# Two activation tiles placed 64 bytes aside from the spacing of the others, in a two-block network of float32 matmuls on one core

## The chip, the cores and the metric

The kernel runs on one core of one Trainium2 chip. The metric is the time of one execution on the device in microseconds; the number for the kernel before is the median of three runs. A profile is one execution, taken apart by the hardware profiler; its span goes from the first to the last instruction, and its own time lies a little above its span.

## The reference

A token block of 256 x 1024 float32 goes through two networks, one after the other. The first has one layer: a feed-forward, a mixer (softmax attention with a forget gate beside a chunked delta rule), a cross-attention to a memory of 256 tokens, and a second feed-forward. The second has two layers: a feed-forward, a mixer (a short convolution beside a state-space scan), a feed-forward, and a gated embedding. There are six feed-forwards in all, of one form:

```python
def swiglu(x, w_gate, w_up, w_down):
    return (jax.nn.silu(x @ w_gate) * (x @ w_up)) @ w_down
```

with 1024 inputs, 2816 inner features and 1024 outputs. Nearly all of the arithmetic is in such products of the activations with weights of 1024 to 2816 rows, all float32.

## The kernel before

Activations are kept transposed: features on the 128 partitions, the 256 tokens along the row. An activation of 1024 features is eight tiles, the 2816 inner features are NF = 22 tiles. A product in full float32 is made of three products in the faster type fp32r: each operand is split into a rounded part (hi) and the rest (lo), and hi x hi, hi x lo and lo x hi are added up in PSUM.

Weights come in units of up to four blocks of 128 x 256. `wunit` (line 284) loads a unit into a tile `raw` by a DMA issued from the sync engine's queue, ScalarE rounds it into a tile `hi` (line 298), VectorE subtracts to get `lo` (line 299). There are four `raw`, three `hi` and three `lo` tiles of 4096 bytes a partition, in turns.

An activation that enters a product is split into a tile of the arena `R`: 2048 bytes a partition, the rounded part in the first 1024 bytes, the rest in the second. `mm3` (line 326) makes the three matmuls of one block: the weights are held in TensorE (128 x 128, 512 bytes of a partition), the activation streams past them (256 columns):

```python
wh, wl = (q[:, m0:m0 + P] for q in w)
xh, xl = x[:, 0, :], x[:, 1, :]
self.mm(ps, wh, xh, first, False)
self.mm(ps, wh, xl, False, False)
self.mm(ps, wl, xh, False, last)
```

All of them are recorded on line 266. `block` (line 338) goes through the K input tiles four at a time (one unit), and within the four, first for one half of 128 output features and then for the other, tile by tile. So a pass over eight input tiles is 48 matmuls, in which each tile has three in a row, twice; a pass over 22 inner tiles is 132. In `proj_tok` (two projections per mixer and memory) the roles are swapped: the activation is held and hi or lo stream. `preload` splits the first weight blocks of some stages into R tiles ahead of time, so in four short stretches both operands of a matmul are R tiles.

A feed-forward (`ffn`, line 471) makes 11 units of gate and up, 22 passes over its eight input tiles, and writes 22 inner tiles; then four passes over these for the down projection. Each matmul pass waits for its weights by semaphores; TensorE takes its instructions in the order in which the program's planner has put them.

The arena `Arena` (line 97) hands out tiles. `add` makes n tiles in a pool, named by the arena and a running number: `R` has 20 outer tiles r0 to r19 from the start, and every feed-forward opens a scope (line 459) with NF = 22 inner ones, which lie behind the outer ones in the same memory each time (r20 to r41 in the first, r42 to r63 in the second, r64 to r85 in the third, then r90, r112 and r138 and on). `get` hands out the front of the free list, `put` appends to its end, new tiles go to the front. So a feed-forward's inner activation is the 22 inner tiles in order, and its inputs are outer tiles as the free list has them.

Followed through the program, r1 is one of the eight inputs in the first, second, third and sixth feed-forward and not in the fourth and fifth, and serves for one of the inputs in other stages; 746 matmuls stream it. 144 stream the fifth inner tile of a feed-forward (24 in each).

The pools lay their tiles down one after another in each partition. By the sizes of the tiles in the order of the program (bytes from the start of a partition): the three `hi` begin at 42112, 46208 and 50304, the three `lo` at 54400, 58496 and 62592, r0 at 119104 and r1 at 121152, r19 at 158016, the first inner tile at 160064, the fifth at 168256. So `hi` and `lo`, and every 512-byte slice of them that is held, begin at a multiple of 128 (at 128 modulo 512), and every R tile begins 64 past one (at 320 modulo 512). A tile named `pad` of 32 bytes, which nothing reads or writes, stands in the constants' pool; its place in the layout stays empty.

Of the kernel before, what the change touches and what calls it, by code (L numbers as in the profile page):

```python
# [8 lines left out]
F32 = mybir.dt.float32  # L9
# [6 lines left out]
P = 128  # L16
# [4 lines left out]
NF = FF // P  # L21
# [75 lines left out]
class Arena:  # L97
# [7 lines left out]
    def add(self, pool, n):  # L105

        new = []
        for _ in range(n):
            nm = f"{self.name}{self.n}"
            new.append(pool.tile(self.shape, self.dtype, tag=nm, name=nm, bufs=1)[:])  # L110
            self.n += 1
        self.free[:0] = new
        self.parts.append(new)
# [1362 lines left out]
```

## Time and profile before

| | us |
|---|---|
| runs of the kernel before | 2220.98, 2214.37, 2216.32 |
| their median | 2216.32 |
| the profiled execution, its own time | 2218.59 |
| its span | 2216.8 |
| TensorE (PE) busy | 2195.6 |
| VectorE (DVE) busy | 1558.2 |
| ScalarE (ACT) busy | 1185.7 |
| GpSimd (POOL) busy | 43.7 |

Busy times of different engines lie beside each other and don't add up. A matmul's duration in the profile is from its start to a modelled end; matmuls are pipelined, the next starts while this one still runs, so 99% busy says that PE is never without work and not that it is at its peak. In the lists, "x1483" is a count and "281" after a busy time is the mean duration of one in ns. An entry of the form `pm<-r,hi` is a matmul into a PSUM tile pm from an R tile and a hi tile; buffer numbers are left out, so the rows don't tell r1 from r0.

### The profile page before, as it was taken

To read this page: it belongs to the slowest core of one execution; us is meant where nothing else is said; L and a number is where in the kernel's file an instruction comes from. 1 tells how busy PE (TensorE), PEld (TensorE's weight loads), DVE (VectorE), ACT (ScalarE), POOL (GpSimd) and SP (SyncE) were. 2 spreads that over 40 slices of the span, in tenths; PEclk is the share of its full clock that TensorE was granted. 3 is DMA by queue.
4 is the path that set the end of the run, shared out by engine and by line. 5 is a ranking of instruction groups with operands and counts; after the bars stand their busy time and mean duration, and the time that the engine had idled before them with its cause. 6 is when DMAs were issued, how large, how long until landed. Compare 5 with 4: busy or idle time off the path is not lost.

```text
span 2216.8 us, 45480 instructions
## 1 busy us (share of the span) xinstructions
PE 2195.6 (99%) x18672; PEld 2153.5 (97%) x18672; DVE 1558.2 (70%) x2608; ACT 1185.7 (53%) x2033; POOL 43.7 (2%) x54
## 2 busy tenths in 40 slices
PE   8999999999999999999999999999999999999998
PEld 8999997999999999998999999999999999999998
DVE  7756873667665766798766766676669876767666
ACT  6545633555444544567555555454457755645444
POOL 1000000000000000000000000000000000000000
PEclk9999997999999999999999999999999999999999
DMA  7565520535566556553455656656665436566563
GB/s 256 177 188 166 166 77 1 172 124 162 189 184 192 173 185 184 188 179 105 157 189 184 193 191 193 189 186 193 191 199 184 135 126 194 178 195 192 193 189 126
DMA packets 110369, 379.44 MB, mean 171 GB/s; under 512 B 12368, under 2 KB 17104, under 8 KB 110160
## 3 DMA queue, kind: packets, MB, share of 16 engines
q1 hardware_dynamic: 110160, 376.53, 53.6%
q8 instruction: 146, 2.39, 0.5%
q14 instruction: 63, 0.52, 0.1%
HBM read 375.43 MB, written 1.05 MB: 170 GB/s over the span
## 4 chain that ended last, share of the span: by engine, by line
PE 96%; DVE 2%; ACT 1%; DMA 1%; issue 0%; POOL 0%; SPq 0%; DVEq 0%; ACTq 0%; POOLq 0%
PE pm L266 84%; PE px L266 11%; PE px L269 1%; DVE lo L299 0%; DVE s L260 0%; DMA raw<-in_ffn_w_gate_dram 0%; DMA raw<-in_ple_w_gate_dram 0%; ACT hi L298 0%; DMA raw<-in_ffn_wu_dram 0%; ACT d L263 0%; PE pm L269 0%; ACT L263 0%; DVE r L260 0%; DVE w L254 0%; DVE w L260 0%
## 5 line engine op out<-in xcount | busy, mean ns | idle before, releaser
L266 PE MATMUL pm<-r,hi 128*128 128x256 f32 x10640 | 1864.0, 280 | 7.5 <-ACT hi L298 5.7
L266 PEld LDWEIGHTS pm<-r,hi 128*128 128x128 f32 x10640 | 1625.1, 189 | 9.8 <-ACT hi L298 5.7
L266 PE MATMUL pm<-r,lo 128*128 128x256 f32 x5320 | 1485.3, 279 | 0.0
L299 DVE TENSOR_TENSOR lo<-raw,hi 128x1024 fp32r<-128x1024 f32 (+1 forms) x718 | 860.9, 1199 | 488.9 <-ACT hi L298 485.6
L298 ACT CAST hi<-raw 128x1024 fp32r<-128x1024 f32 (+1 forms) x718 | 739.3, 1030 | 732.7 <-PE pm L266 576.7
L266 PEld LDWEIGHTS pm<-r,lo 128*128 128x128 f32 x5320 | 1002.1, 188 | 1.2 <-issue 0.7
L277 ACT CAST r<-w 128x256 fp32r<-128x256 f32 x136 | 54.5, 403 | 60.4 <-DVE w L254 60.3
L254 DVE TENSOR_TENSOR t<-pm,rb 128x512 f32<-128x512 f32 (+1 forms) x132 | 80.4, 635 | 0.2
L263 ACT ACTIVATE r<-s,vec 128x256 fp32r<-128x256 f32 x136 | 66.0, 504 | 21.4 <-DVE s L260 17.9
L263 ACT ACTIVATE sq<-s 128x256 f32<-128x256 f32 x152 | 60.4, 411 | 28.1 <-DVE s L254 19.8
L260 DVE SCALAR_TENSOR_TENSOR s<-pm,vec,s 128x255 f32<-128x255 f32 x144 | 68.9, 479 | 2.8
L260 DVE SCALAR_TENSOR_TENSOR r<-s,vec,r 128x256 fp32r<-128x256 f32 x136 | 65.3, 498 | 4.9 <-ACT r L263 4.4
L266 PE MATMUL px<-r,hi 128*128 128x256 f32 x384 | 66.9, 279 | 0.0
L278 DVE TENSOR_TENSOR r<-w,r 128x256 fp32r<-128x256 f32 x136 | 57.0, 421 | 8.1
L266 PEld LDWEIGHTS px<-r,hi 128*128 128x128 f32 x384 | 58.6, 189 | 0.0
L266 PE MATMUL px<-r,lo 128*128 128x256 f32 x192 | 53.5, 278 | 0.0
L414 POOL TENSOR_TENSOR rs<-rv,mhalf 128x2 f32<-128x2 f32 x26 | 23.4, 900 | 1505.0 <-DVE rv L412 1505.0
L263 ACT ACTIVATE w<-t 128x256 f32<-128x256 f32 x132 | 48.1, 409 | 7.2 <-DVE t L254 7.2
L254 DVE TENSOR_TENSOR w<-w,t 128x256 f32<-128x256 f32 x132 | 50.1, 418 | 0.3 <-ACT w L263 0.2
L266 PE MATMUL px<-d,d 128*64 128x128 f32 (+2 forms) x384 | 42.7, 291 | 0.3 <-DVE d L254 0.2
L257 DVE TENSOR_TENSOR acc<-acc,sq 128x256 f32<-128x256 f32 x94 | 39.4, 419 | 4.6 <-ACT sq L263 1.9
L263 ACT ACTIVATE d<-px,nac 128x128 f32<-128x128 f32 x128 | 36.5, 376 | 3.1 <-PE px L266 2.8
(231 smaller groups left out, 1369.2 us busy)
## 6 DMA issues: line engine op xcount, KB each, us to landing
raw<-in_w_in_dram SPq DMA_DIRECT2D x188, 512.0 KB, 3.7
raw<-in_ffn_wg_dram SPq DMA_DIRECT2D x88, 512.0 KB, 4.4
raw<-in_ffn_wu_dram SPq DMA_DIRECT2D x88, 512.0 KB, 4.3
raw<-in_ffn_wd_dram SPq DMA_DIRECT2D x80, 512.0 KB, 4.0
raw<-in_ffn_w_up_dram SPq DMA_DIRECT2D x44, 512.0 KB, 4.5
raw<-in_ffn_w_gate_dram SPq DMA_DIRECT2D x43, 512.0 KB, 4.5
raw<-in_ffn_w_down_dram SPq DMA_DIRECT2D x40, 512.0 KB, 3.8
raw<-in_m_w_out_dram SPq DMA_DIRECT2D x32, 512.0 KB, 4.3
```

The source lines that it names most:

```text
L254: self.nc.vector.tensor_tensor(out=out, in0=a, in1=b, op=ALU.mult)
L257: self.nc.vector.tensor_tensor(out=out, in0=a, in1=b, op=ALU.add)
L260: self.nc.vector.scalar_tensor_tensor(out=out, in0=a, scalar=s, in1=b, op0=op0, op1=op1)
L263: self.nc.scalar.activation(out, a, f, **kw)
L266: self.nc.tensor.matmul(out, lhsT=lhsT, rhs=rhs, start=start, stop=stop)
L269: self.nc.tensor.transpose(out, a, self.ident[:k, :k])
L277: nc.scalar.copy(hi, src)
L278: nc.vector.tensor_tensor(out=lo, in0=src, in1=hi, op=ALU.subtract)
L298: nc.scalar.copy(o, r)
L299: nc.vector.tensor_tensor(out=d, in0=r, in1=o, op=ALU.subtract)
L414: self.nc.gpsimd.tensor_tensor(out=r, in0=v, in1=self.mhalf[:, :2], op=ALU.pow)
```

## The change

When the arena `R` gets its 20 outer tiles, a tile of 16 float32 (64 bytes a partition) is set into the pool ahead of r1 and another ahead of r2. When it gets 22 inner tiles, one is set ahead of the fifth and another ahead of the sixth. Nothing reads or writes these tiles. So r1 and the fifth inner tile of each feed-forward stand 64 bytes further from the tile before them than the others do, and everything behind the second pad stands 128 bytes further on than it did, behind all four 256 bytes. In the new layout r1 begins at 121216, a multiple of 128 (384 modulo 512); r2 to r19 and the first four inner tiles begin 64 past one (448 modulo 512); the fifth inner tile begins at 168448, a multiple of 128 (0 modulo 512); the later ones 64 past one (64 modulo 512). `hi` and `lo`, which lie ahead of the arena, stay where they are.

```diff
@@ -105,8 +105,10 @@
     def add(self, pool, n):
 
         new = []
-        for _ in range(n):
+        for j in range(n):
             nm = f"{self.name}{self.n}"
+            if self.name == "r" and j in {20: (1, 2), NF: (4, 5)}.get(n, ()):
+                pool.tile([P, 16], F32, tag=f"pad{nm}", name=f"pad{nm}", bufs=1)
             new.append(pool.tile(self.shape, self.dtype, tag=nm, name=nm, bufs=1)[:])
             self.n += 1
         self.free[:0] = new
```

## Rows read from the trace of the kernel before

**Rows 1.** The page: the span, the busy time of each engine, and the chain of work that ended last by engine; from its 40 slices the clock that TensorE was granted, in tenths of full speed (9 is 90% or more).
```profile
span 2216.8 us, 45480 instructions
...
PE 2195.6 (99%) x18672; PEld 2153.5 (97%) x18672; DVE 1558.2 (70%) x2608; ACT 1185.7 (53%) x2033; POOL 43.7 (2%) x54
...
PEclk9999997999999999999999999999999999999999
...
PE 96%; DVE 2%; ACT 1%; DMA 1%; issue 0%; POOL 0%; SPq 0%; DVEq 0%; ACTq 0%; POOLq 0%
```

**Rows 2.** The two largest groups of PE's matmuls over the whole span, each shape by itself: names and shapes, count, busy us, mean ns of one, idle us before them and what ended it.
```profile
L266 PE MATMUL pm<-r,hi 128*128 128x256 f32 x10640 | 1864.0, 280 | 7.5 <-ACT hi L298 5.7 <-ACT r L263 1.1 <-DVE r L260 0.7
L266 PE MATMUL pm<-r,lo 128*128 128x256 f32 x5320 | 1485.3, 279 | 0.0
```

**Rows 3.** The same groups in two windows of 60 us: first 60 to 120 us (three rows, the last of them a spread of row factors), then 1300 to 1360 us (two rows).
```profile
L266 PE MATMUL pm<-r,hi 128*128 128x256 f32 x340 | 60.3, 281 | 0.0
L266 PE MATMUL pm<-r,lo 128*128 128x256 f32 x170 | 47.8, 281 | 0.0
L266 PE MATMUL px<-con,rs 128*128 128x128 f32 x2 | 0.4, 274 | 0.0
...
L266 PE MATMUL pm<-r,hi 128*128 128x256 f32 x354 | 60.2, 276 | 0.0
L266 PE MATMUL pm<-r,lo 128*128 128x256 f32 x178 | 49.1, 276 | 0.0
```

**Rows 4.** Busy time of each engine in five windows: start and end, length, then for each engine its busy us with the count of instructions that run in the window, the granted clock, the DMA engines' busy share and GB/s.
```profile
24.00:200.00 176.00, 174.62 (x1483) 174.42 (x1483) 115.97 (x165) 86.69 (x131) 1.62 (x1) 1.00 0.61 191
530.00:719.00 189.00, 188.99 (x1606) 188.79 (x1605) 124.16 (x179) 92.40 (x142) 0.70 (x1) 1.00 0.59 183
740.00:920.00 180.00, 180.00 (x1531) 180.00 (x1530) 116.20 (x156) 87.81 (x129) 2.57 (x1) 1.00 0.60 186
940.00:1009.00 69.00, 69.00 (x587) 68.80 (x586) 63.38 (x116) 46.37 (x74) 0.00 (x0) 1.00 0.57 180
1500.00:1650.00 150.00, 150.00 (x1326) 150.00 (x1325) 96.96 (x128) 73.36 (x105) 0.00 (x0) 1.00 0.63 194
```

**Rows 5.** Instructions of PE in order of time, like ones merged (start us, us, line and names, count): around 1746 us, and then around 1152 us.
```profile
1745.78 0.40 PE L266 MATMUL pm<-r,hi 128*128 128x256 f32 x2
...
1746.13 0.40 PE L266 MATMUL pm<-r,hi 128*128 128x256 f32 x2
1746.36 0.62 PE L269 MATMUL px<-con,s 128*128 128x128 f32 x4
...
1747.30 0.39 PE L266 MATMUL pm<-r,hi 128*128 128x256 f32 x2
...
1747.64 0.39 PE L266 MATMUL pm<-r,hi 128*128 128x256 f32 x2
...
1151.61 0.39 PE L266 MATMUL pm<-r,hi 128*128 128x256 f32 x2
...
1151.95 0.39 PE L266 MATMUL pm<-r,hi 128*128 128x256 f32 x2
...
1152.29 0.50 PE L266 MATMUL px<-ones,acc 128*128 128x1 f32 x4
...
1153.09 0.40 PE L266 MATMUL pm<-r,hi 128*128 128x256 f32 x2
...
1153.44 0.40 PE L266 MATMUL pm<-r,hi 128*128 128x256 f32 x2
```

**Rows 6.** The stretch in which R tiles stream past R tiles without interruption: the merged instruction list from its start to the matmul behind it, and its group in the window 1470 to 1475.7 us.
```profile
1470.12 5.92 PE L266 MATMUL pm<-r,r 128*128 128x256 f32 x48
1475.88 0.40 PE L266 MATMUL pm<-r,hi 128*128 128x256 f32 x2
...
L266 PE MATMUL pm<-r,r 128*128 128x256 f32 x47 | 5.8, 283 | 0.0
```

**Rows 7.** The group of matmuls with lo in windows around the four stretches of R against R: ahead of the undisturbed one (1465.5 to 1469.5 us), behind it (1476 to 1481 us), and behind the other three (449.6 to 452, 534.8 to 540 and 731.4 to 736 us).
```profile
L266 PE MATMUL pm<-r,lo 128*128 128x256 f32 x13 | 3.6, 276 | 0.0
...
L266 PE MATMUL pm<-r,lo 128*128 128x256 f32 x11 | 3.1, 281 | 0.0
...
L266 PE MATMUL pm<-r,lo 128*128 128x256 f32 x5 | 1.4, 281 | 0.0
...
L266 PE MATMUL pm<-r,lo 128*128 128x256 f32 x10 | 2.4, 281 | 0.0
...
L266 PE MATMUL pm<-r,lo 128*128 128x256 f32 x8 | 2.0, 281 | 0.0
```

**Rows 8.** Groups of matmuls in six windows: with hi in 1111 to 1151 and 1209 to 1275 us, with lo in 1389 to 1449 us, with hi in 1595 to 1661, 1936 to 2009 and 2012 to 2184 us.
```profile
L266 PE MATMUL pm<-r,hi 128*128 128x256 f32 x237 | 40.4, 276 | 0.0
...
L266 PE MATMUL pm<-r,hi 128*128 128x256 f32 x387 | 66.2, 276 | 0.0
...
L266 PE MATMUL pm<-r,lo 128*128 128x256 f32 x177 | 48.9, 276 | 0.0
...
L266 PE MATMUL pm<-r,hi 128*128 128x256 f32 x388 | 66.3, 276 | 0.0
...
L266 PE MATMUL pm<-r,hi 128*128 128x256 f32 x429 | 73.3, 276 | 0.0
...
L266 PE MATMUL pm<-r,hi 128*128 128x256 f32 x950 | 161.6, 276 | 0.0
```

## The prediction

> **What bounds the kernel now.** I read the page first [rows 1]: TensorE is busy for 2195.6 of 2216.8 us and the chain that ended last is 96% PE, with the granted clock at full in nearly every slice. No wait is worth removing; only the time of one matmul can move the end. Then I read the costliest matmuls [rows 2]: 15,960 of the 18,672 are the 256-column products of an activation tile (r, streamed) with weights (hi, lo, held) into one of the two PSUM pools; with the other pool and the swapped and small forms the program has 17,040. Their mean duration, 279 and 280 ns, is no price, since they are pipelined. The price is the distance from one start to the next, so I took windows with little else on PE. The reader is to see that the same instruction runs at two speeds, at the same full clock [rows 3, 4]. From 60 to 120 us the rows have a mean of 281 ns and some 510 matmuls, from 1300 to 1360 us 276 ns and 532. With the windows of [rows 4], less the 2.4 at the edges that a window counts too many (a matmul of 281 or 276 ns overlaps the next two): 180 us / 1528.6 = 117.8 ns against 150 us / 1323.6 = 113.3 ns. The difference is 4.4 ns, or 3.9%.
>
> Which speed rules isn't the work's doing: DVE, ACT and DMA are about as busy per us in the last row of [rows 4] as in the one of 180 us. The speed is kept for 180 us and more, and changes at an interruption. At 1746.4 us four transposes come between the matmuls, and the steps of three, 0.35 us before, are 0.34 us within a microsecond after; at 1152.3 us four small sums come between, and the steps go from 0.34 to 0.35 us [rows 5]. So there are two locked rhythms, call them slow and fast. Three of the six feed-forwards run slow, 24 to 200, 530 to 719 and 740 to 920 us; the later three run fast but for moments.
>
> There is a third speed. Four short stretches hold weights in R tiles and stream R tiles against them. In the undisturbed one 48 matmuls take from 1470.12 to 1475.88 us, 120.0 ns each, at a mean of 283 ns [rows 6]. What is different there is the address. By the layout told above hi and lo start at 0 modulo 128 bytes and every R tile at 64; in those stretches both operands start at 64. So equal remainders cost 120 ns, unequal ones 113.3 or 117.8 ns.
>
> **The change part by part.** It adds no instruction, wait or transfer: nothing reads or writes the pads. It puts r1, and the fifth inner tile of each feed-forward, at 0 modulo 128, where hi and lo are; the pad behind each brings the rest back to 64. All tiles behind move by 128 or 256 bytes, which leaves their remainder alone; I cost that at nothing. If their distance modulo 512 mattered too, both speeds already occur at two such distances, 320 where an r streams and 192 where hi or lo streams against r (proj_tok), so nothing speaks for a cost.
>
> The direct cost: following get and put through the program, the two kinds are streamed 746 and 144 times. In each feed-forward that has r1 among its inputs (the first, second, third and sixth) that is 11 units x 2 weights x 2 halves x 3 = 132, and for the inner tile in all six 4 x 2 x 3 = 24. The trace of before has no matmul with both operands at 0, so I bound its price: 120.0 ns as in [rows 6], 6.7 above fast, or 113.3 as fast, no loss. Below fast nothing shows a gain. 890 x 6.7 ns = 5.9 us is the upper end, 0 the lower; between ends that nothing tells apart I take half, 3 us.
>
> The indirect effect is the larger one. A slow stretch is slow because each matmul repeats the one before with the same address relation. The odd tile breaks the repetition, six matmuls of every 48 in a unit with r1 (three in a row, twice), and six of every 132 in the down projection. In the slow first three feed-forwards it comes back in each of 22 passes and in each of 4. If the break lets them fall into the fast rhythm, as the interruption at 1746.4 us did, the three windows of 1483 + 1606 + 1531 matmuls [rows 4], some 4550 of them of the plain kind, gain 4550 x 4.4 ns = 20.0 us. The slow matmuls of the mixers, which meet no odd tile in their stretch, gain nothing. Sum: -20 + 3 = -17 us. The profiled execution took 2218.6 us (span 2216.8 and 1.8 around it), 2.3 above the median of 2216.3; -17 makes it 2201.6 there and 2199 at the median. No cover is used up: what waits for PE on DVE and ACT has 30% and 47% of idle time [rows 1].
>
> A rule speaks against any effect. What the rows show is that two matmul streams with different addresses differ by 6.7 ns [rows 3, 6]. The Trainium skill, "SBUF — State Buffer", section "SBUF: two separate sides", says that PE never waits on anyone on the engine side, and "TensorE: Matmul & The Clock Gate", section "Step-by-step: what each phase is for", gives the moving operand and the weights a read port each; by them an address would cost nothing and the time would stay, which is the second rival below. The 120 ns differ from that.
>
> **The rivals.** *The break makes slow, not fast* (slower). For it: the stretches with equal remainders are the only breaks by address that the trace has, and what follows each is slow. The undisturbed one came out of fast matmuls (276 ns) and left slow ones (281 ns); after the others it is 281 too [rows 7]. If three matmuls with the odd tile do what 48 did, every fast stretch with an odd tile turns slow there, until an interruption frees it. Those of [rows 8] are 40, 66, 60, 66, 73 and 172 us, 477 us together, and 3.9% of it is 19 us; short ones left out and the slow feed-forwards, which pay 468 x 2.2 ns = 1 us more, make it 21. That gives 2216 + 21 = 2237; if nothing frees it, fast stretches without an odd tile (as 1300 to 1360 us [rows 3] and the first 95 us of the last window of [rows 4], some 400 us in all, an estimate) add 16 us, up to some 2253. Against it: in those stretches the two operands start at the same place modulo 512 too, while the odd tiles stand 256 (r1) and 128 (inner) away from the weights, so it is not the same relation; and three matmuls are not 48. It decides as soon as the odd tile's own matmuls take 120 ns and the next ones 117.8.
>
> *Nothing happens* (the same): the rhythm is set by interruptions alone, or the pads don't move the tiles, or the odd tile is no break. Then it is 2216, with 3 us at most for the odd tiles. For it: the interruptions stay where they are, and a spread's two matmuls between 60 and 120 us change nothing [rows 3]. Against it: 120 ns shows that addresses count. The existing pad in the constants leaves its hole in the layout, so the new ones will too.
>
> *All becomes fast*: the slow parts of the mixers as well, where the longest, 940 to 1009 us, has 587 matmuls [rows 4] and the others together some three times as many, an estimate from the slow parts of the timeline: 2,300 x 4.4 = 10 us more, and 2189. It needs breaks where no odd tile is; a corner of the first case.
>
> **How the numbers follow.** Faster in the three slow feed-forwards, 2199, with its own range of 2186 (all fast, no direct cost: 2189 - 3) to 2209 (some half of it): 0.50. The break makes slow, 2237 (2224 to 2253): 0.33. Nothing, 2216: 0.17. What decides between the first two is whether the relation modulo 128 alone counts, which the trace can't tell; I lean to the first, since the odd tile's relation is one that the trace has not shown to be slow, and since most of its uses, 468 of 890, are in slow stretches, where it can lose only 2.2 ns each. A measurement of this kernel can tell about 0.3% (6.6 us) from no change. Range: 2188 to 2242, which leaves out the corner below and the longer half of the slower case above, under 2 in 10. Faster 0.50, same 0.17, slower 0.33.
>
> **What would show it.** Right: in the windows of the first three feed-forwards the mean duration is 276 ns and the count per 180 us goes from 1531 to near 1590; the last feed-forward stays at 276. The steps at the odd tile show its own price, 0.34 or 0.36 us for three. Wrong: 281 ns in the last feed-forward, or from 1389 to 1449 us, where it is 276 now: then the break makes slow. If each stretch keeps its speed, nothing happened. What would make the number wrong though the mechanism is right: a break that frees only the up and gate half (two thirds of a feed-forward), or only the down half.

## The result and the profile after

The change made the kernel slower by 0.6%: 2233.36 us, the median of five runs from 2223.17 to 2237.41, against 2218.66 us of five of the kernel before, ratio 1.0061 (95% interval 1.0033 to 1.0089). The forecast was 2199. The profiled execution took 2230.09 us with a span of 2228.3. The lines that answer to [rows 1 and 2], from the page and from the list of PE's groups:

```profile
span 2228.3 us, 45480 instructions
...
PE 2207.3 (99%) x18672; PEld 2167.6 (97%) x18672; DVE 1559.8 (70%) x2608; ACT 1185.1 (53%) x2033; POOL 43.3 (2%) x54
...
PE 96%; DVE 2%; ACT 1%; DMA 1%; issue 0%; POOL 0%; SPq 0%; DVEq 0%; ACTq 0%; POOLq 0%
...
L268 PE MATMUL pm<-r,hi 128*128 128x256 f32 x10640 | 1881.3, 280 | 6.7 <-ACT hi L300 5.7 <-DVE r L262 0.7 <-ACT r L265 0.3
```

The program has the same instructions in the same numbers, and the span grew by about what PE's busy time grew (11.5 and 11.7 us): the matmuls themselves are slower, nothing waits more. (The line numbers are two higher because the edit adds two lines.) The windows of [rows 4] after the change, columns as there:

```profile
24.00:200.00 176.00, 174.63 (x1488) 174.42 (x1487) 116.37 (x166) 87.16 (x131) 1.62 (x1) 0.99 0.63 192
530.00:719.00 189.00, 188.22 (x1609) 187.68 (x1609) 123.45 (x177) 91.18 (x140) 1.39 (x2) 1.00 0.61 189
740.00:920.00 180.00, 180.00 (x1544) 180.00 (x1543) 116.11 (x153) 87.55 (x126) 3.29 (x2) 1.00 0.61 188
940.00:1009.00 69.00, 69.00 (x604) 68.36 (x603) 66.33 (x116) 49.83 (x79) 0.00 (x0) 1.00 0.57 184
1500.00:1650.00 150.00, 150.00 (x1288) 150.00 (x1287) 95.70 (x127) 71.43 (x103) 0.00 (x0) 1.00 0.60 188
```

Read the count of PE, the number behind the first x. The third feed-forward goes from 1531 only to 1544, where 1590 was forecast; the fifth, which ran fast and whose gate and up part streams no odd tile at all (a tile set 64 bytes aside: r1, or a fifth inner tile), falls from 1326 to 1288, that is from 113.3 to 150 us / 1285.6 = 116.7 ns. The part of this window without an odd tile, 1500 to 1570 us, is shown by itself below; it is slow. So a large loss lies where no odd tile is. Places that the forecast named, by the mean of one (hi in 1300 to 1360, lo in 1389 to 1449, hi in 2012 to 2184 us; 276 in all three before, [rows 3, 8]):

```profile
L268 PE MATMUL pm<-r,hi 128*128 128x256 f32 x354 | 60.3, 276 | 0.0
...
L268 PE MATMUL pm<-r,lo 128*128 128x256 f32 x173 | 47.9, 277 | 0.0
...
L268 PE MATMUL pm<-r,hi 128*128 128x256 f32 x930 | 160.8, 278 | 0.0
```

The last feed-forward is neither fast (276) nor slow (281), the fourth keeps its speed, and its down projection loses a little. To see stretches of one kind I use five windows that lie in one stage in all of the kernels, all but the second: gate and up of the third feed-forward (740 to 840 us), its down projection (866 to 914; the stage ends at 909 after the change and at 899 in the run e10 below), gate and up of the fifth (1500 to 1570), a mixer (1820 to 1900), gate and up of the sixth (2025 to 2100). First before, then after:

```profile
740.00:840.00 100.00, 100.00 (x852) 100.00 (x851) 67.43 (x90) 48.04 (x72) 0.00 (x0) 1.00 0.59 188
866.00:914.00 48.00, 48.00 (x410) 48.00 (x409) 26.46 (x36) 22.95 (x31) 0.00 (x0) 1.00 0.61 183
1500.00:1570.00 70.00, 70.00 (x620) 70.00 (x619) 47.64 (x63) 34.46 (x50) 0.00 (x0) 1.00 0.62 195
1820.00:1900.00 80.00, 80.00 (x706) 80.00 (x704) 56.04 (x84) 43.66 (x67) 0.81 (x1) 1.00 0.60 192
2025.00:2100.00 75.00, 75.00 (x664) 75.00 (x663) 51.83 (x69) 36.95 (x56) 0.00 (x0) 1.00 0.61 195
```

```profile
740.00:840.00 100.00, 100.00 (x852) 100.00 (x851) 67.55 (x88) 47.33 (x70) 0.00 (x0) 1.00 0.59 188
866.00:914.00 48.00, 48.00 (x420) 48.00 (x419) 28.75 (x38) 24.41 (x36) 2.60 (x1) 1.00 0.64 192
1500.00:1570.00 70.00, 70.00 (x597) 70.00 (x596) 46.30 (x62) 33.64 (x49) 0.00 (x0) 1.00 0.58 186
1820.00:1900.00 80.00, 80.00 (x682) 80.00 (x681) 50.97 (x73) 40.31 (x59) 0.81 (x1) 1.00 0.58 185
2025.00:2100.00 75.00, 75.00 (x655) 75.00 (x654) 50.58 (x68) 36.65 (x53) 0.00 (x0) 1.00 0.59 190
```

The counts take few values: 620 or 597 is 113.3 or 117.7 ns (70 us over the count less 2.4), and 706 or 682 in 80 us are the same two steps. The down projection with its odd tile gained a little (410 to 420), the slow gate and up passes with r1 gained nothing, and two fast stretches without an odd tile turned slow. What they have in common is the term costed at nothing: every tile behind the first pad moved.

### The profile page after: what moved, and what is told of

The parts are those of the page before. It is cut to its first block, busy times and chain, and to the rows that moved or that the text cites. A ratio compares the mean times of both kernels' runs of the same rounds, so it can differ in the third digit from the quotient of the medians.

```text
span 2228.3 us, 45480 instructions
## 1 busy us (share of the span) xinstructions
PE 2207.3 (99%) x18672; PEld 2167.6 (97%) x18672; DVE 1559.8 (70%) x2608; ACT 1185.1 (53%) x2033; POOL 43.3 (2%) x54
## 4 chain that ended last, share of the span: by engine, by line
PE 96%; DVE 2%; ACT 1%; DMA 1%; issue 0%; POOL 0%; SPq 0%; DVEq 0%; ACTq 0%; POOLq 0%
PE pm L268 84%; PE px L268 11%; PE px L271 1%; DVE lo L301 0%; DVE s L262 0%; ACT hi L300 0%; DMA raw<-in_ffn_w_up_dram 0%; DMA raw<-in_ffn_wu_dram 0%; DMA raw<-in_ple_w_proj_dram 0%; DVE r L262 0%; PE pm L271 0%; DVE acc L259 0%; ACT d L265 0%; ACT L265 0%; DVE w L256 0%
```

## The experiments

Distances below are the start of the held slice less the start of the streamed tile, modulo 512 bytes. Before, it is 320 for every R tile with weights. The change leaves r0 at 320, puts r1 at 256, r2 to r19 and the first four inner tiles at 192, the fifth inner tile at 128 and the later ones at 64. "Slow" and "fast" are the two rhythms of the prediction, 117.8 and 113.3 ns from start to start. The theories named in the expectations: A, the odd tile's break reshuffles what is carried on; B, the distance of the shifted tiles decides; C, chance in each execution.

**The parts of the change.** Each edit stands in `add` (pads ahead of the tile named, in floats of 4 bytes):

```diff
 e1  outer: 16 ahead of r1, 16 ahead of r2
 e2  inner: 16 ahead of the fifth, 16 ahead of the sixth
 e3  outer: 32 ahead of r1; inner: 32 ahead of the fifth
 e4  outer: 16 ahead of r0
 e14 outer: 32 ahead of r1
```

e1, r1 alone odd: 

> Only r1 is odd; everything behind it stands 128 bytes further on, the inner tiles with it, and no inner tile is odd. Theory A (what an odd tile does to the rhythm is carried on until the next interruption, and so reshuffles which stretches run fast): the part of the loss that comes from r1, +5 to +15 us against before (2224 to 2234); the down projections keep one rhythm within a pass, since nothing breaks them there. Theory B (the odd tiles matter little; the shift of all tiles behind them by 128 bytes, from a distance of 320 to one of 192 modulo 512 to the weights, decides): +12 to +18 us, 2231 to 2237, as with all four pads. Theory C (the rhythm of each stretch is chance, drawn anew in each execution): anywhere from 2215 to 2237, with runs of one kernel as far apart as two kernels.

e2, the fifth inner tile alone odd: 

> Only the fifth inner tile of each feed-forward is odd; the 20 outer tiles and the first four inner ones stand where they stood before. Theory A: in the down projections of the first three feed-forwards the tiles behind the odd one run at 113.3 ns, as they do with all four pads (some 1200 matmuls x 4.4 ns = -5 us), and in the later three the odd tile costs 72 x 6 ns = +0.4 us; what the stretches behind carry on is open, so 2208 to 2222. Theory B: the inner tiles behind the odd one stand at another distance, the rest does not, 2214 to 2222. Theory C: anywhere from 2215 to 2237.

e3, the shift without odd tiles: 

> One tile of 128 bytes ahead of r1 and one ahead of each fifth inner tile: every tile stands where the two pads before it put it, except r1 and the fifth inner tile, which stand 64 past a multiple of 128 like all others. So the shift is there and the odd tiles are not. Theory A: as before, 2215 to 2222, with the map of fast and slow stretches of the kernel before. Theory B: as with the change, 2228 to 2237, with stretches that were fast before and have no odd tile (1120 to 1195, 1482 to 1596, 1803 to 1935 us) slow. Theory C: anywhere between, and its runs some 14 us apart.

e4, everything at equal remainders: 

> One tile of 64 bytes ahead of r0: every R tile begins at a multiple of 128, as hi and lo do, so that every matmul has both operands at the same remainder. If equal remainders cost 120.0 ns a matmul whatever their distance modulo 512 (the R tiles against R tiles of the prediction): 9961 fast ones x 6.7 ns + 6717 slow ones x 2.2 ns = +81 us, 2300. If only an equal place modulo 512 costs it (here the distance is 256): as any other distance, 2215 to 2237, with 113.3 and 117.8 ns side by side. With all four pads r1, at this very distance, took 117.7 ns in the mean among tiles at other distances, between the two.

e14, the shift alone, run later: 

> One tile of 128 bytes ahead of r1 and nothing else: r1 to r19 and all inner tiles at 192 from the weights, no odd tile. If the distance of 192 is the whole of the loss, with R or the weights moved alike: 2231 to 2237, as with the weights moved (2233.8), and as with r1 odd on top of it (2233.6), so that the odd r1 neither costs nor gains there. If the shift without odd tiles (2241.8) showed the loss of a moved R: 2238 to 2245, and then the odd r1 gains 8 us there.

| kernel | us, median | runs | ratio to before (95%) |
|---|---|---|---|
| e14, r1 and all behind it at 192, none odd | 2245.57 | 6 | 1.0112 (1.0084 to 1.0139) |
| e3, as e14, later inner tiles at 64 | 2241.77 | 6 | 1.0107 (1.0077 to 1.0138) |
| e1, as e14, r1 odd (256) | 2233.64 | 12 | 1.0070 (1.0045 to 1.0095) |
| e2, inner pads alone, later inner tiles at 192 | 2225.49 | 12 | 1.0022 (1.0001 to 1.0042) |
| e4, all at equal remainders (256) | 2292.73 | 6 | 1.0339 (1.0311 to 1.0366) |

Theory B came out in kind: the shift without any odd tile costs more than the whole change, 25 us in e14. Its numbers were not met throughout: e3 lies above the 2228 to 2237 that B gave it, the fifth feed-forward, which it had slow in e3, stayed fast there, and e2 lies above what A and B gave it (2222 at most). On top of the shift the odd r1 takes 9 to 12 us off (e1 against e14, which differ in r1's place alone; by the ratios or by the medians). Theory A had expected before's time for e3, and falls as the cause of the loss. e14 in the last three of the five windows (the first two count 853 and 410, slow as before):

```profile
1500.00:1570.00 70.00, 70.00 (x620) 70.00 (x619) 48.44 (x64) 34.20 (x50) 0.00 (x0) 1.00 0.61 194
1820.00:1900.00 80.00, 80.00 (x682) 80.00 (x681) 51.27 (x73) 39.88 (x57) 0.00 (x0) 1.00 0.59 187
2025.00:2100.00 75.00, 75.00 (x641) 75.00 (x640) 49.40 (x69) 35.03 (x51) 0.70 (x1) 1.00 0.58 186
```

The mixer (682) and the last gate and up passes (641, 75 us / 638.6 = 117.4 ns) are slow with no odd tile in the kernel. The fifth feed-forward is fast here: not every stretch follows the shift in the same way.

The tiles of a pass, told apart by the order of the program, show one reason. The shift leaves r0 behind, at 320 among tiles at 192, and r0 is an input just where r1 is: in the first, second, third and sixth feed-forward. The inputs of the sixth come in the order r0 to r3, twice, then r16 to r19, twice. With the change, the first matmuls of r19, r0, r1, r2, r3 and r0 again:

```profile
2054.78 0.39 PE L268 MATMUL pm<-r,hi 128*128 128x256 f32 x2
...
2055.12 0.40 PE L268 MATMUL pm<-r,hi 128*128 128x256 f32 x2
...
2055.48 0.40 PE L268 MATMUL pm<-r,hi 128*128 128x256 f32 x2
...
2055.83 0.40 PE L268 MATMUL pm<-r,hi 128*128 128x256 f32 x2
...
2056.18 0.39 PE L268 MATMUL pm<-r,hi 128*128 128x256 f32 x2
...
2056.52 0.40 PE L268 MATMUL pm<-r,hi 128*128 128x256 f32 x2
```

The three matmuls take 0.34 us with r19, 0.36 with r0, 0.35 with r1 and r2 and 0.34 with r3. In the mean over the later units r0 takes 117.7 ns a matmul, r1 119.0, r2 116.7, the other five 113.3. In e14, where r1 stands at 192 like the others, r0 takes 115.7 and all the others 117.7 or 117.8. In e6 below, where r0 stands at 192 as well, all eight take 113.3. So in this stage r0, which nobody meant to set aside, ends the fast rhythm in each pass, and the odd r1 brings it back. In the second and third feed-forward, where the other tiles run slow, r1 does not: all eight stay between 116.7 and 119.2 ns.

In e4 all matmuls with weights run at one speed, the price that was taken from [rows 6]; in 1620 to 1690 us, where PE has nothing but 256-column products:

```profile
1620.00:1690.00 70.00, 70.00 (x585) 70.00 (x585) 40.80 (x55) 32.20 (x45) 0.00 (x0) 1.00 0.61 182
```

70 us / 582.6 = 120.2 ns. Its median, 2292.7, is 73 us above before, against 81 expected.

**The distance, made by moving the weights.** R stays; constants of 128 or 256 bytes are allocated behind the weights instead of ahead of them:

```diff
 e6, e8
-        self.ones = {n: self.cst.tile([P, 1], F32, name=f"ones{n}") for n in (1, 128, 512, 1024)}
+        self.ones = {n: self.sc.tile([P, 1], F32, tag=f"ones{n}", name=f"ones{n}", bufs=1) for n in (1, 128, 512, 1024)}
 e7, e8
-        self.identb = self.cst.tile([P, P], BF16, name="identb")
+        self.identb = self.sc.tile([P, P], BF16, tag="identb", name="identb", bufs=1)
```

e6: 

> R tiles where they stood before; four small constants (128 bytes together) go from ahead of the weights to a place between the weights and R, so that hi and lo stand 128 bytes further ahead and all matmuls with weights go from a distance (held less streamed) of 320 to one of 192 modulo 512. No odd tile. Theory B: as with all tiles shifted, 2232 to 2246. If the place of R itself modulo 512 decides, or the growth of the arena, not its distance to the weights: as before, 2213 to 2226. Theory C: 2213 to 2245 without a rule.

e7: 

> The same with a constant of 256 bytes: hi and lo 256 bytes further ahead, distance 64 modulo 512 for all matmuls with weights. With the shift and no odd tile the inner tiles at that distance took 115.2 ns, those at 192 in the same run 116.8, and with all four pads 113.9 against 116.4. Theory B: 17,000 x (115.2 to 113.9) against the 116.3 of the kernel before in the mean: 19 to 41 us less, 2179 to 2201. Theory C: as before, 2213 to 2226.

e8: 

> Both groups of constants moved, 384 bytes: distance 448 modulo 512 for all matmuls with weights. No run has shown this distance yet. Theory B: anything from 2190 (all at 113.3) to 2247 (all at 117.8), but not the same as both 192 and 64. Theory C: as before, 2213 to 2226.

Measured: 192, 2233.76 us, 1.0056 (1.0032 to 1.0080); 64, 2221.28, 0.9991 (0.9965 to 1.0018); 448, 2234.56, 1.0058 (1.0033 to 1.0083). So 64 is as good as 320, and 448 as bad as 192, with R in its place and no odd tile: the distance itself costs 12 to 13 us in this kernel. B held in kind, its forecast for 64 (2179 to 2201) did not. The constants that were moved are not the cause: the four small ones that e6 and e8 move are moved in e9, e10 and e13 below as well, which are faster than before, and e14 is slow without moving any. In the mixer's window PE counts 706 at 320 and at 64, and 681 and 683 at 192 and 448; e1, e3 and e14 have 683, 681 and 682. In the fifth feed-forward's window e6 counts 596 and e8 620, and e2, whose outer tiles stand at 320 as before, 597; so there the distance of its own tiles doesn't decide, and what does is not shown.

**The price by itself.** 

> The kernel before, and behind its last step a measuring part: 190 passes of 48 matmuls of the usual form, hi and lo held, R tiles streamed, with one to four transposes between passes. The held slice begins 0, 64, 128, 192, 256, 320, 384 or 448 bytes further on than usual (ten passes each), then 32, 96 and 16 bytes; then the first eight again with a DMA, a ScalarE rounding and a VectorE subtraction of a unit beside each pass. The R tiles stand at 320, the weights at 128 modulo 512, so held less streamed is 320 modulo 512 with no offset and goes up with it. The part is no piece of the reference and its time is read from its own stretch. Theory B (distance modulo 512 decides): equal remainders modulo 128 (offsets 64, 192, 320, 448) 120.0 ns at any distance; of the others 320 mostly 113.3, 192 (offset 384) mostly 117.8, and 64 and 448 on one side or the other. Theory C (chance alone): the four unequal distances have the same share of slow passes. If DMA, ScalarE or VectorE bring the slow rhythm, the part without them is 113.3 throughout. For the offsets that aren't multiples of 64, 120 ns or more.

A pass in the part is held hi, hi, lo against streamed rounded, rest, rounded, as in `mm3`, the offset `d` added to the held slice:

```diff
+        q = (k % 3) * S + f * P + d
+        wh, wl = hi[:, q:q + P], lo[:, q:q + P]
```

The loads of the last eighty passes waited for nothing and ran beside the first forty; so the comparison with and without DMA, ScalarE and VectorE is there with the order turned round. In the list of instructions in order of time, of the fifth pass at distances 320 and 448 (offsets 0 and 128), the starts of two triples that are 39 matmuls apart:

```profile
2237.66 0.39 PE L266 MATMUL pm<-r,hi 128*128 128x256 f32 x2
...
2242.08 0.39 PE L266 MATMUL pm<-r,hi 128*128 128x256 f32 x2
...
2353.51 0.40 PE L266 MATMUL pm<-r,hi 128*128 128x256 f32 x2
...
2358.10 0.40 PE L266 MATMUL pm<-r,hi 128*128 128x256 f32 x2
```

4.42 and 4.59 us over 39: 113.3 and 117.7 ns. By the mean of the last 39 steps of each pass, 320 is fast in 19 of 20 passes, 64 in 16 of 20, 192 and 448 in none of 40. Equal remainders take 119.9 or 120.0 at 0 and 256, but 118.6 to 118.8 at 128 and 384 (three first passes, 120.0, apart), where 120.0 had been expected at all four. Offsets of 32, 96 and 16 bytes take 117.3 to 120.1, never 113.3. Load makes no difference: the first four distances (320, 384, 448 and 0) repeat their speeds when it is gone, but for one slow pass at 320.

**What an odd tile does.** 

> The kernel before and behind it a measuring part: passes of 96 matmuls, each pass first 24 at one offset of the held slice, then 72 at another, with one to four transposes between passes, eight passes of each of nine cases. 24 at distance 448 (slow in the first measuring part, 117.8) then 72 at 320 (fast there, 113.3): if the rhythm is a state that is carried on, the 72 stay at 117.8; if the distance sets it, they are 113.3. 24 at 320 then 72 at 448: carried on 113.3, set by distance 117.8. The same with every eighth tile of the 72 odd, as r1 in a unit, ahead of a slow and of a fast start: if the odd tile breaks the slow lock, the matmuls behind it are 113.3 from the first or second odd tile on, also where 448 or 192 are the others' distance; if it throws the rhythm either way, the fast start loses as much as the slow one gains. An odd tile costs 1.4 to 6.7 ns a matmul itself by the first part.

First from 448 (slow) to 320, at 2312.22 us; then from 320 (fast) to 448, at 2413.37:

```profile
2311.86 0.40 PE L266 MATMUL pm<-r,hi 128*128 128x256 f32 x2
...
2312.22 0.39 PE L266 MATMUL pm<-r,hi 128*128 128x256 f32 x2
...
2312.56 0.39 PE L266 MATMUL pm<-r,hi 128*128 128x256 f32 x2
...
2413.37 0.39 PE L266 MATMUL pm<-r,hi 128*128 128x256 f32 x2
...
2413.71 0.39 PE L266 MATMUL pm<-r,hi 128*128 128x256 f32 x2
...
2420.85 0.39 PE L266 MATMUL pm<-r,hi 128*128 128x256 f32 x2
```

The triples go from 0.36 to 0.34 us at the very matmul at which the distance changes, so an address can lift the slow rhythm; and a fast stretch stays fast at 448 for all 72, in seven of seven passes, so 448 is not slow by itself. Neither sets the rhythm alone: one of five slow starts stayed slow at 320, and the eight passes of plain 320 in this part were all slow (117.8), where the first part had it fast. Over all cases the 24 matmuls at the start of a pass ran fast in 20 of 40 passes at 320 and in 13 of 32 at 448, so the first part's sharp preference by distance does not come back here. Then the odd tile as in the change (256 among 192), in a fast pass:

```profile
2860.06 0.40 PE L266 MATMUL pm<-r,hi 128*128 128x256 f32 x2
...
2860.42 0.39 PE L266 MATMUL pm<-r,hi 128*128 128x256 f32 x2
...
2860.76 0.39 PE L266 MATMUL pm<-r,hi 128*128 128x256 f32 x2
```

Its own triple takes 0.36 us, the next one 0.34 again: it pays 6.7 ns a matmul and breaks nothing; in a slow pass the others stay at 117.8 to 118.1 in the mean. At 384 among 320 it is different. A slow start, then a fast one, 69 matmuls each:

```profile
2491.89 0.40 PE L266 MATMUL pm<-r,hi 128*128 128x256 f32 x2
...
2499.95 0.40 PE L266 MATMUL pm<-r,hi 128*128 128x256 f32 x2
...
2583.50 0.39 PE L266 MATMUL pm<-r,hi 128*128 128x256 f32 x2
...
2591.56 0.39 PE L266 MATMUL pm<-r,hi 128*128 128x256 f32 x2
```

8.06 us in both, 116.8 ns: it mixes the two rhythms, whatever came before (116.5 to 116.9 in all sixteen passes). At 0 among 320 the passes end slow (117.8 to 118.0) from either start. So what an odd tile breaks hangs on its own distance and on that of the others.

**The odd tiles with the distance kept.** Pads in floats, on top of e6 (weights 128 bytes ahead) or on before:

```diff
 e9  on e6:     outer 16 ahead of r1, 16 ahead of r2; inner 48 ahead of the fifth, 16 of the sixth
 e10 on e6:     outer 16 ahead of r1, 16 ahead of r2
 e11 on before: inner 16 ahead of the fifth, 48 of the sixth
 e13 on e6:     outer as e10; inner as e11
```

e9: 

> The odd tiles of the change, and every other tile but r0 kept at 64 or 320 from the weights (modulo 512), the distances of the kernels at 2221: weights 128 bytes further ahead as in the run with weights at 192, 64 bytes ahead of r1 and of r2, 192 ahead of the fifth inner tile and 64 ahead of the sixth. r1 stands at 128, the fifth inner tile at 384, both at equal remainders modulo 128; r0 is at 192. Theory B1 (the step of the prediction that failed is only the shift costed at nothing; the odd tile breaks the slow lock as was said): the predicted 17 us off, 2199 to 2209, or by the difference between all four pads and the shift alone (2241.8 - 2233.4) 8 us off, 2211 to 2216. Theory B2 (the odd tile's break gains only where the others stand at 192 or 448; elsewhere it throws as many stretches out of the fast rhythm as into it): 2219 to 2230.

e10: 

> The same with r1 alone odd (at 128 from the weights) and everything behind it at 64; r0 at 192. B1: the gate and up passes of the first, second and third feed-forward (3 x 1056 matmuls that were slow) go to 113.3 ns, less 528 odd ones at up to 6.7 more: 2206 to 2214. B2: 2219 to 2230, and the last feed-forward, fast before, mixed.

e11: 

> The layout of before with only the fifth inner tile odd (64 bytes ahead of it, at 256 from the weights) and 192 bytes behind it, so that the later inner tiles stand at 64 and not at 192. With the inner pads of the change alone (later inner tiles at 192) the time was 2225.5, 1.0022 of before. If the tiles at 192 were the loss there: 2212 to 2220, down projections of the first three feed-forwards at 113.3 ns behind the odd tile. If the odd tile itself is: 2222 to 2230.

e13: 

> The run with r1 alone odd and the weights moved (2210.5) with the fifth inner tile odd as well, this time as in the run with it alone (2213.1): 64 bytes ahead of it, 192 behind. It stands at 0 from the weights, the first four inner tiles at 64, the later ones at 320. If the two gains are of different passes and add up: 2222 - 11 - 8 = 2203, within 2199 to 2207. If the inner tile's own relation decides (0 here, 256 there): 2209 to 2214, as the run with both odd tiles (2212.4), where the inner tile's matmuls took 120.1 ns.

Measured: e9 2212.37 us, 0.9955 (0.9935 to 0.9975); e10 2210.48, 0.9943 (0.9922 to 0.9964); e11 2213.09, 0.9953 (0.9936 to 0.9970); e13 2210.44, 0.9954 (0.9936 to 0.9971). All four beat the kernels before and after: with the others' distance at 64 or 320, an odd tile does gain. The gains don't add up: e10 and e11 free the same down projections, and e13 is not below e10. e10 in three of the windows (740, 866, 2025), then e11 in 866:

```profile
740.00:840.00 100.00, 100.00 (x868) 100.00 (x867) 68.53 (x91) 49.29 (x73) 0.00 (x0) 1.00 0.60 190
866.00:914.00 48.00, 48.00 (x422) 47.84 (x422) 32.66 (x48) 26.14 (x39) 3.29 (x2) 1.00 0.64 195
...
2025.00:2100.00 75.00, 75.00 (x652) 75.00 (x651) 50.33 (x68) 36.53 (x53) 0.00 (x0) 1.00 0.60 190
```

```profile
866.00:914.00 48.00, 48.00 (x425) 48.00 (x424) 29.24 (x38) 24.91 (x37) 2.59 (x1) 1.00 0.64 192
```

868 is 115.5 ns, half way between slow and fast (883 would be fast), and the tiles tell what it is made of. In e10 r1 stands at 128 and r0 at 192 among tiles at 64; the inputs of the third feed-forward are r10, r11, r14 and r15, twice, then r0 to r3, twice. The first matmuls of the last r15, r0 and r1 of a pass, then of the last r3 and of the next r10 and r11:

```profile
791.43 0.39 PE L269 MATMUL pm<-r,hi 128*128 128x256 f32 x2
...
791.77 0.40 PE L269 MATMUL pm<-r,hi 128*128 128x256 f32 x2
...
792.12 0.40 PE L269 MATMUL pm<-r,hi 128*128 128x256 f32 x2
...
794.24 0.40 PE L269 MATMUL pm<-r,hi 128*128 128x256 f32 x2
...
794.59 0.39 PE L269 MATMUL pm<-r,hi 128*128 128x256 f32 x2
...
794.93 0.39 PE L269 MATMUL pm<-r,hi 128*128 128x256 f32 x2
```

The four tiles without r0 and r1 run at 113.3 ns, the four with them at 117.2 to 118.1: the fast rhythm ends at r0 again (0.34 us, then 0.35) and is back behind the last r3. So half of each pass is freed where all of it was slow (868 for 852), and half is lost where all of it was fast (652 for 664, the sixth). Which of r0 and r1 does what here was not tried apart: no run has r1 odd and r0 at 64. In e10 the down projection that follows is fast with no odd tile in it; in e11 it is freed by its own odd tile and the step from 320 to 64 behind it (425). With a step from 320 to 192 behind the same odd tile (e2) it is not freed (411).

**The change once more.** 

> The change itself once more, beside these two: 2229 to 2237 (ratio to before 1.0033 to 1.0089). If the rhythm of a stretch is drawn anew in each execution, its map of fast and slow stretches differs from the first one's though the program is the same; if the layout fixes it, the map is the same.

2231.19 us, 1.0037 (1.0018 to 1.0057). Below, the time of each stage in one profiled execution: from the start of its first matmul to the start of the next stage's first, the same matmuls in each kernel. "Rest 1" is what lies between the first feed-forward and the second, "rest 3" and "rest 5" (the mixers of the second network) what follows the third and the fifth; "others" is what follows the second, the fourth and the sixth, up to the last product with weights. The column of before is the time, the others the difference to it, all in us:

| stage | before | change | again | e14 | e3 | e2 | e6 | e10 | e11 |
|---|---|---|---|---|---|---|---|---|---|
| gate, up 1 to 3 | 386.5 | +1.0 | -0.4 | +0.8 | +0.8 | -3.3 | -0.7 | -6.3 | 0.0 |
| down 1 to 3 | 186.6 | -4.6 | -4.6 | 0.0 | -1.9 | -0.2 | 0.0 | -7.0 | -6.2 |
| gate, up 4 | 120.6 | 0.0 | 0.0 | +0.3 | +0.3 | 0.0 | 0.0 | 0.0 | 0.0 |
| gate, up 5 | 121.9 | +3.9 | +3.9 | -0.4 | -0.4 | +4.3 | +3.9 | -0.2 | 0.0 |
| gate, up 6 | 120.6 | +1.7 | +1.7 | +4.3 | +4.3 | 0.0 | 0.0 | +2.3 | 0.0 |
| down 4 to 6 | 179.5 | +2.1 | +2.1 | +2.3 | +2.1 | +7.0 | +2.3 | 0.0 | +0.5 |
| rest 1 | 328.2 | -2.4 | -2.4 | +2.8 | +2.9 | +1.1 | +2.4 | -2.2 | +1.3 |
| rest 3 | 351.7 | +1.4 | +4.0 | +5.8 | +3.3 | +0.2 | +2.9 | -0.2 | -0.1 |
| rest 5 | 349.2 | +6.4 | +6.5 | +8.7 | +8.7 | +0.3 | +5.4 | +2.1 | +2.5 |
| others | 53.9 | +2.4 | +1.5 | +1.2 | +1.3 | +0.4 | +1.5 | +1.0 | +0.3 |

The same program repeats its stages to 0.1 us in seven of the ten rows. Theory C falls as the account: the layout fixes most of what runs fast. (In the first execution of the change TensorE's granted clock was 0.91 in the mean of 60 to 80 us, 1.00 the second time; that is the +1.0 against -0.4 of the first row. e14 had 0.92 there.) Some stretches do differ (rest 3), and runs of one kernel lie up to 1% apart.

## Why the prediction was wrong

**What bounds the kernel, and the three speeds: right.** PE's own rhythm is the time, before and after. 113.3 and 117.8 ns came back in the unequal kernels, and e4 shows 120 as the price of equal remainders at a distance of 256; at 128 and 384 the measuring part has 118.6 to 118.8. The forecast named a rule against an effect of addresses. The Trainium skill, "SBUF — State Buffer", section "SBUF: two separate sides", says that PE never waits on anyone on the engine side; that an address would then cost nothing was an inference of the forecast, and e4's 73 us and the 120.0 ns of the measuring part differ from it.

**The step that failed: "All tiles behind move by 128 or 256 bytes, which leaves their remainder alone; I cost that at nothing."** It is the largest term: +25 us with no odd tile (e14), +12 to +13 with the weights moved instead (e6, e8). The ground given, that both speeds occur at 320 and at 192, was true and no argument: that both occur at a distance says nothing of how much of the time each rules there. The mixers (rest 3 and 5) have few odd matmuls even with the change, and lost 14.5 us in e14, which has none. So most of the 15,960 matmuls of [rows 2] went to a distance that the forecast had not priced, for the sake of 890 odd ones. The same step overlooked that r0 does not move with the others: in the sixth feed-forward the loss begins at r0 in each pass.

**The direct cost: 3 us, between 0 and 5.9.** The upper bound was the right price for the pair in the change where the others are fast (0.36 for 0.34 us, 6.7 ns), and lower in slow stretches. It is small, as said.

**The indirect gain: right in kind, mis-sized, -20 us.** Its ground, that a slow stretch is slow because each matmul repeats the address relation of the one before, was read from no row: the fast stretches of before repeat the same 320. What came out is that an odd tile can lift the slow rhythm, but only at some distances. The change gained 4.6 us in the three slow down projections, of some 7 to be had (e10); 1.9 of it come without odd tiles too (e3). In gate and up of the slow feed-forwards it gained nothing that both executions show, since r1 at 256 among tiles at 192 lifts nothing there, nor in the measuring part (e12); in the sixth it does, and 1.7 us are lost there instead of e14's 4.3. With r1 at 128 and r0 at 192 among tiles at 64 half of each pass is freed, -6.3 us of some 14 (3168 x 4.4 ns). The feed-forwards 1 to 3 then gain 13.3 us together (e10), and the sixth loses 2.3. That the odd r1 gains on the whole is shown among tiles at 192: 9 to 12 us (e1 against e14). The 11 to 13 us of e10 against before, where all tiles at 64 are no faster than before (e7), belong to r0 and r1 together.

**The rival "the break makes slow": its time, 2237, was near by luck, its mechanism was not the one.** By it the loss lies in fast stretches with an odd tile. Losses are there, 1.7 us in the last gate and up passes and 2.1 in the down projections 4 to 6, where 4.6 and 7 would be a fall to slow; but e3, with the same shift and no odd tile, loses 4.3 and 2.1 in the same places. Nearest to the rival comes e2, whose down projections 4 to 6 all fall to slow (+7.0); there the tiles behind the odd one stand at 192, and with them at 64 (e11) it is +0.5. The fifth gate and up passes and most of the mixers have no odd tile, and the kernel without any odd tile is the slowest of the unequal ones. "Nothing happens" and "all becomes fast" are out. The measured 2233 lies in the stated range only because that range was drawn wide enough to hold this rival; the direction was the other one.

**Open.** Why moving R (e14) costs twice what moving the weights to the same distance (e6) does. By the stages the sixth feed-forward is 4.3 us slower in e14, which is r0's doing as seen above, and the fifth 4.3 faster; what is left is some 6 us in the mixers (rest 3 and 5), where r0 is streamed by 96 of 5376 matmuls of the kind in [rows 2]. r0 at 320 among tiles at 192 is one difference; no run moves it along with the others to 192. Nor is it shown why a stretch at 192 or 448 mostly runs slow in the kernel and in the first measuring part, or why plain 320 was slow in the second.

## What to carry to other kernels

A pad moves everything behind it and nothing ahead of it: before an edit is costed by the tile that it is meant for, list what else changes its place, and against what, and make the control that has the shift alone. Where a matmul stream is the bound, look at the step from start to start against the addresses of both operands; in this kernel equal remainders modulo 128 cost 3.4% of the time, and 192 or 448 against 64 or 320 modulo 512 cost 0.6%, for no instruction at all. One inner tile of 22 set aside, with the tiles behind it at 64, gave 0.5% (e11).

## What the runs showed of the hardware that was not expected

The rhythm of fp32r matmuls of 256 columns is a state: at one granted clock, 1.00, and one distance, 320, stretches of hundreds of matmuls ran at 113.3 or at 117.8 ns (before, 740 to 840 and 1500 to 1570 us), and a change of the address of one operand switched it within one matmul (2312.22 us). Offsets of 16, 32 or 96 bytes never reached 113.3 (117.3 to 120.1). A single tile at another distance than its neighbours can end the fast rhythm or bring it back, in pass after pass (r0 and r1 in the sixth feed-forward). The state is so repeatable that a second execution of the same program had most of its stages within 0.1 us, while kernels that differ by 128 bytes in one place differ by 25.
